# Dilated queries, keys and eight gate tiles as 2x2 block products with seven multiplications instead of eight

## The chip, the cores and the metric

The kernel runs on one core of one Trainium2 chip. The metric is the device time of one execution in microseconds (us). A core has five engines with an instruction stream each: TensorE (PE in the profile; its weight loads are listed as PEld), VectorE (DVE), ScalarE (ACT), GpSimd (POOL) and SyncE (SP), which issues the transfers here. Each runs its stream in order, and waits on semaphores for the others. Matrix products are made by PE into PSUM banks of 128 partitions x 512 float32; operands lie in SBUF.

## The reference

One layer of an encoder in float32, for one sequence of 1024 tokens and a width of 1024. `proj` is one input projection that is cut into ten parts: two mixers, their output gates z, and two merge gates g.

```python
h = rmsnorm(x, attn_norm_g)
c_q, c_kv, k_rope, z_mla, q_dil, k_dil, v_dil, z_dil, g_mla, g_dil = split(h @ w_in)
a_out = mla_attention(c_q, c_kv, k_rope, ...)          # 8 heads, dense, 1024 x 1024
y_mla = (a_out * silu(z_mla)) @ w_o_mla
d_out = dilated_mixture(rope(q_dil), rope(k_dil), v_dil)  # 3 groups x 8 heads of 64,
                                                       # windows 128, 512, 2048, dilations 1, 4, 16
y_dil = (d_out * silu(z_dil)) @ w_o_dil
merged = sigmoid(g_mla + b1) * y_mla + sigmoid(g_dil + b2) * y_dil
out = rmsnorm(x + merged @ w_out, final_norm_g)
```

## The kernel before

**Products.** Each float32 operand is split into a high part in the format fp32r and a low part, the rest (`split`, L73 to L76: a cast on ACT, L75, and a subtraction, L76, on POOL for weights and on DVE or POOL elsewhere). A product is three matmuls, high x high, low x high and high x low (`mm3`, L69 to L71; in a projection L70 takes the low part of the activations and L71 that of the weights). One mm3 of 128x512 is called a step here. A projection of one weight tile (128 output columns, a contraction of 1024 = 8 steps) for one half of the tokens (512) is eight steps into one bank.

**Stages.** The program goes through five stages; the times are those of the profiled execution. 0 to 241 us: latent projections, tables, norm factors, and the values of the dilated mixer (`dil_v`). 241 to 491 us: `dil_qk`, the dilated queries and keys, twelve calls of two weight tiles each, so 48 banks of 24 matmuls; a call makes for each half of the tokens two banks `pj`, rotates them (`rope`, four multiplications on DVE, L233, and two additions on POOL, L234 and L235), splits the result into `dq_st` for groups 0 and 1 (L75 and L76 on ACT and POOL) or copies it for group 2 (ACT, L397), and writes it to DRAM in pieces of 128 KB. 491 to 815 us: dilated attention, four head pairs of three groups each, and a combination of the groups per pair (`combine`). 815 to 1195 us: dense attention (`mla_attention`). 1195 us to the end: `output`.

**Fillers.** `fillers` (L415) is a generator of steps that don't depend on the attention at hand. It first makes the 24 tiles of z and of the gates, 16 steps each (numbers 4 to 7, 0 to 3, 16 to 23, 8 to 15; a DVE multiplication L428, a tanh on ACT, for z two POOL operations L431 and L432, a store to `s_zs` or `s_gt`), then the output projection of the dilated mixer (64 steps), then that of the dense mixer without its last quarter ("early" merges, three steps and a POOL addition for each of 16 pieces), as far as it gets before the attention ends. FIRST_FEED steps come ahead of the dilated attention; after that `feed(FEED[i])` draws steps from it after each group of scores or transposes: FEED[0] to FEED[5] in the dilated attention, FEED[6] and FEED[7] in the dense one. They use one PSUM bank, `pj`.

**Output.** For each of 16 pieces (8 tiles of columns x 2 halves of tokens) what is left of the dense mixer's projection is made: four steps, or one if the piece was early. DVE multiplies it by the gate (L830), POOL adds the dilated part (L831), ACT casts (`m`) and DVE subtracts (`mg_l`, L76). Beside each piece one of 16 parts of `w_out` is loaded (`wo_raw`) and split (ACT `wout_h`, DVE `wout_l`, L76). Then come 384 matmuls of 128x512 of the final product, the residual, the norm and the stores.

**Order.** The order in each engine's stream is set by a scheduler that takes the program as written, the free buffers of the pools and a model of times; it can bring an instruction forward past others of its engine. PSUM has eight banks: six and two for `pj` before the attention, and then two for transposes (`pt`), one for `av`, four for scores (`s_ps`) and one for `pj`. The attention takes over the banks when the pools of the stage before are closed.

## Time and profile before

| | us |
|---|---|
| median of 3 runs | 1338.19 (1333.47 to 1341.69) |
| profiled execution | 1334.28 |
| its span, first to last instruction | 1332.5 |
| 0 to 241: latents, tables, values | 241 |
| 241 to 491: queries and keys | 250 |
| 491 to 815: dilated attention | 324 |
| 815 to 1195: dense attention | 380 |
| 1195 to 1332.5: output | 137.5 |

The profiled execution is the basis of every sum; 1.8 us of it lie outside the span, and it is 3.9 us below the median. Rows of a table of windows give the stretch, its length, then for PE, PEld, DVE, ACT and POOL the busy time and the number of instructions, then the clock that PE was granted (1.00 is full), the mean busy share of the DMA engines and GB/s. Rows of groups give the line in the code, engine, operation, result and operands with shape, the count, the busy time, the mean duration in ns, and the idle time of that engine just before, with what ended it. Rows of a timeline give start, duration, instruction and the idle time before it.

### The profile page before, as it was taken

To read this page: it belongs to the slowest core of one execution; us is meant where nothing else is said; L and a number is where in the kernel's file an instruction comes from. 1 tells how busy PE (TensorE), PEld (TensorE's weight loads), DVE (VectorE), ACT (ScalarE), POOL (GpSimd) and SP (SyncE) were. 2 spreads that over 40 slices of the span, in tenths; PEclk is the share of its full clock that TensorE was granted. 3 is DMA by queue.
4 is the path that set the end of the run, shared out by engine and by line. 5 is a ranking of instruction groups with operands and counts; after the bars stand their busy time and mean duration, and the time that the engine had idled before them with its cause. 6 is when DMAs were issued, how large, how long until landed. Compare 5 with 4: busy or idle time off the path is not lost.

```text
span 1332.5 us, 19561 instructions
## 1 busy us (share of the span) xinstructions
PE 1275.5 (96%) x7101; PEld 1108.2 (83%) x7101; DVE 670.5 (50%) x1340; ACT 577.7 (43%) x1230; POOL 454.9 (34%) x302
## 2 busy tenths in 40 slices
PE   8999999999999999989999989999999999998998
PEld 8898999888888878877878777788888878886786
DVE  7473520222222215666475666766665666658622
ACT  6533332223322336545455453565555545454322
POOL 2251212676466634425422040312111022045522
PEclk9999999999999999989999999999999999999999
DMA  9758563575435435688777777625342463136322
GB/s 324 220 167 303 183 231 107 154 217 139 125 104 157 136 105 155 161 197 205 195 202 202 196 200 187 188 98 166 80 117 82 103 193 112 59 117 206 130 94 76
DMA packets 128256, 213.06 MB, mean 160 GB/s; under 512 B 36440, under 2 KB 65696, under 8 KB 126304
## 3 DMA queue, kind: packets, MB, share of 16 engines
q1 hardware_dynamic: 128160, 211.81, 54.8%
q8 instruction: 56, 0.92, 0.3%
q14 instruction: 40, 0.33, 0.1%
HBM read 143.01 MB, written 68.75 MB: 159 GB/s over the span
## 4 chain that ended last, share of the span: by engine, by line
PE 64%; DMA 12%; DVE 6%; issue 3%; SPq 2%; ACT 1%; POOL 0%; DVEq 0%; ACTq 0%; POOLq 0%
PE pj L69 15%; PE pj L71 15%; PE pj L70 15%; PE pt L546 3%; DMA op_a<-s_dk 2%; PE av L555 2%; PE av L554 2%; SPq L65 2%; DMA s_sd<-av_t 2%; PE s_ps L69 2%; PE s_ps L70 2%; PE s_ps L71 2%; PE pt L647 1%; DMA gate<-s_zs 1%; PE av L668 1%
## 5 line engine op out<-in xcount | busy, mean ns | idle before, releaser
L69 PE MATMUL pj<-hT_h,w_h 128*128 128x512 f32 x768 | 314.9, 410 | 2.2 <-DVE zg_z L428 2.1
L76 POOL TENSOR_TENSOR w_l<-w_raw,w_h 128x1024 fp32r<-128x1024 f32 (+1 forms) x70 | 167.8, 2399 | 434.6 <-ACT w_h L75 370.2
L71 PE MATMUL pj<-hT_h,w_l 128*128 128x512 f32 x768 | 301.8, 393 | 0.0
L70 PE MATMUL pj<-hT_l,w_h 128*128 128x512 f32 x768 | 301.7, 393 | 0.0
L233 DVE TENSOR_TENSOR rope_m<-pj,cs_d 128x512 f32<-128x512 f32 x96 | 61.8, 686 | 241.2 <-PE pj L71 241.2
L76 DVE TENSOR_TENSOR pt_l<-pt,pt_h 128x512 fp32r<-128x512 f32 x192 | 131.6, 686 | 87.9 <-ACT pt_h L75 86.3
L71 PEld LDWEIGHTS pj<-hT_h,w_l 128*128 128x128 f32 x768 | 145.4, 189 | 31.7
L69 PEld LDWEIGHTS pj<-hT_h,w_h 128*128 128x128 f32 x768 | 145.8, 190 | 27.7 <-DVE zg_z L428 3.0
L70 PEld LDWEIGHTS pj<-hT_l,w_h 128*128 128x128 f32 x768 | 146.2, 190 | 24.8
L75 ACT CAST pt_h<-pt 128x512 fp32r<-128x512 f32 x192 | 112.0, 584 | 116.5 <-PE pt L546 48.2
L70 PE MATMUL pj<-w_l,hT_h 128*128 128x256 f32 x384 | 109.2, 284 | 0.0
L71 PE MATMUL pj<-w_h,hT_l 128*128 128x256 f32 x384 | 109.0, 284 | 0.0
L69 PE MATMUL pj<-w_h,hT_h 128*128 128x256 f32 x384 | 109.0, 284 | 0.0
L75 ACT CAST w_h<-w_raw 128x1024 fp32r<-128x1024 f32 (+1 forms) x70 | 72.3, 1035 | 72.9 <-PE pj L70 59.4
L535 ACT ACTIVATE p<-s_ps,m_nm 128x512 f32<-128x512 f32 x128 | 87.4, 697 | 30.6 <-PE pt L546 19.1
L529 DVE TENSOR_REDUCE m_nm<-s_ps 128x1 f32<-128x512 f32 x128 | 86.6, 685 | 25.3 <-PE s_ps L71 23.1
L613 ACT ACTIVATE p<-p,d_st 128x256 f32<-128x256 f32 x128 | 64.4, 504 | 64.3 <-DVE d_st L612 64.1
L546 PE MATMUL pt<-consts,p 128*128 128x128 f32 x512 | 78.4, 276 | 4.1 <-ACT av_t L577 3.8
L612 DVE CUSTOM_DVE_ANT_0 p<-s_ps,masks 128x256 f32<-128x256 f32 x128 | 50.9, 416 | 47.7 <-PE s_ps L640 25.6
L69 PEld LDWEIGHTS pj<-w_h,hT_h 128*128 128x128 f32 x384 | 73.2, 191 | 1.1
L70 PEld LDWEIGHTS pj<-w_l,hT_h 128*128 128x128 f32 x384 | 73.3, 191 | 0.8
L71 PEld LDWEIGHTS pj<-w_h,hT_l 128*128 128x128 f32 x384 | 73.1, 190 | 0.7
(234 smaller groups left out, 2568.3 us busy)
## 6 DMA issues: line engine op xcount, KB each, us to landing
w_raw<-wt SPq DMA_DIRECT2D x48, 512.0 KB, 4.8
op_b<-s_dq SPq DMA_DIRECT2D x32, 512.0 KB, 8.6
s_dq<-dq_st SPq DMA_DIRECT2D x80, 128.0 KB, 2.5
s_dk<-dq_st SPq DMA_DIRECT2D x80, 128.0 KB, 2.5
gate<-s_gt SPq DMA_DIRECT2D x34, 256.0 KB, 3.1
s_dv<-dv_st SPq DMA_DIRECT2D x32, 256.0 KB, 4.6
s_gt<-zg_t SPq DMA_DIRECT2D x32, 256.0 KB, 2.7
w_raw<-wv SPq DMA_DIRECT2D x12, 512.0 KB, 5.7
```

Of the source, the lines that this page charges most:

```text
L65: self.nc.sync.dma_start(out=out, in_=in_)
L69: mm(out, lh, rh, start=start, stop=False)
L70: mm(out, lh, rl, start=False, stop=False)
L71: return mm(out, ll, rh, start=False, stop=stop)
L75: self.nc.scalar.copy(out=h, in_=raw)
L76: sub.tensor_tensor(out=l, in0=raw, in1=h.bitcast(F32), op=ALU.subtract)
L233: v.tensor_tensor(out=mi, in0=p, in1=tab, op=ALU.mult)
L529: v.tensor_reduce(out=nm[:, hh, qb, kb:kb + 1], in_=s, axis=AX.X, op=ALU.max, negate=True)
L535: nc.scalar.activation(out=p[:, 512 * kb:512 * kb + 512], in_=ss[kb], func=AF.Exp, bias=nm[:, hh, qb, 2:3], accum_out=den[:, hh, qb, kb:kb ...
L546: self.anchor = nc.tensor.transpose(pt[:, o:o + 128], P[b2][:, 128 * kc:128 * kc + 128], self.ident)
L612: nc.vector.tensor_tensor_reduce(out=p, in0=s, in1=mask, op0=ALU.add, op1=ALU.min, scale=-0.125, scalar=3e38, accum_out=nm)
L613: nc.scalar.activation(out=p, in_=p, func=AF.Exp, scale=-1.0, bias=nm, accum_out=den)
```

## The change

A pair of weight tiles, with its contraction cut into two halves of 512 and the tokens into two halves, is a 2x2 block product: each of four results (two tiles x two token halves) is the sum of two block products, eight in all. The changed kernel makes it by the Strassen-Winograd scheme: seven block products of four steps, on sums of blocks. `block_pair` does that for a pair: four sums of weight blocks on POOL, seven splits of a block of 128x512 (ACT cast, POOL subtraction, in place of two splits of 128x1024), seven products of 12 matmuls into four banks `st_a` to `st_d` (two sets of four, so all eight banks), three copies of a bank to SBUF on ACT, and five additions on DVE of which four are in place in PSUM. The sums of the activations, `s0` to `s3`, are made once by `block_sums`: the input is loaded again (16 loads of 256 KB), scaled on ACT, summed on POOL, and split on ACT and DVE.

The twelve calls of `dil_qk` use it, and so do gate tiles 8 to 15, as four pairs (ZG_PAIRS) behind calls 2, 5, 8 and 11; these eight tiles leave the fillers, and FEED is lowered. The rotation is now all on DVE and partly in place in PSUM (two multiplications to SBUF, two in place, two additions in place, for each half), the subtraction of the split of `dq_st` goes from POOL to DVE, and the stores of queries and keys are 512 KB each instead of 128 KB, 40 instead of 160. Weight tiles are split in halves of 128x512 throughout. `dil_v` is called in another order around `block_sums`, the scaling of the cosine and sine tables and the zeroing of a tile come earlier (both on POOL). In the changed file the lines of `mm3` are L71 to L73, the split's subtraction is L78, and the gate product L830 is L931.

```diff
-FEED = (1.9, 1.35, 1.2, 1.25, 2, 3, 1.1, 1.1)
+FEED = (1.4, 1.0, 0.9, 0.95, 1.5, 2.2, 0.95, 0.95)
...
+ZG_PAIRS = ((8, 2), (10, 5), (12, 8), (14, 11))
...
-        h = wp.tile([128, 8, 128], F32R, name="w_h")
-        l = wp.tile([128, 8, 128], F32R, name="w_l")
-        self.split(raw[:, :n], h[:, :n], l[:, :n], self.nc.gpsimd)
+        for k in range(0, n, 4):
+            m = min(4, n - k)
+            h = wp.tile([128, 4, 128], F32R, name="w_h", bufs=bufs)
+            l = wp.tile([128, 4, 128], F32R, name="w_l", bufs=bufs)
+            self.split(raw[:, k:k + m], h[:, :m], l[:, :m], self.nc.gpsimd)
+            w.append((h, l))
...
+    def block_sums(self, sp, tp):
 
         nc, a = self.nc, self.a
...
+        p = nc.gpsimd
+        self.sh = [sp.tile([128, 4, 512], F32R, name=f"s{i}_h") for i in range(4)]
+        self.sl = [sp.tile([128, 4, 512], F32R, name=f"s{i}_l") for i in range(4)]
+        for kc in range(4):
+            y = {}
+            for i in range(2):
+                for k in range(2):
+                    x = y[i, k] = tp.tile([128, 512], F32, name=f"y{i}{k}", bufs=2)
+                    c = kc + 4 * k
+                    self.dma(x, a["xt"][i, :, c])
+                    nc.scalar.mul(x, x, self.ga[:, c:c + 1])
+
+            p.tensor_tensor(out=y[1, 1], in0=y[1, 0], in1=y[1, 1], op=ALU.add)
+            p.tensor_tensor(out=y[1, 0], in0=y[0, 0], in1=y[1, 0], op=ALU.subtract)
+            p.tensor_tensor(out=y[0, 0], in0=y[1, 1], in1=y[0, 0], op=ALU.subtract)
+            p.tensor_tensor(out=y[0, 1], in0=y[0, 1], in1=y[0, 0], op=ALU.subtract)
+            for i, x in enumerate((y[1, 1], y[0, 0], y[1, 0], y[0, 1])):
+                self.split(x, self.sh[i][:, kc], self.sl[i][:, kc], nc.vector)
...
+    def block_pair(self, first, tp, pp):
+
+        nc, a = self.nc, self.a
+        p, v = nc.gpsimd, nc.vector
+        raw = []
+        for i, wp in enumerate((self.wp, tp)):
+            raw.append(wp.tile([128, 8, 128], F32, name="w_raw", bufs=2))
+            self.dma(raw[i], a["wt"][first + i])
+        b = {(k, i): raw[i][:, 4 * k:4 * k + 4] for k in range(2) for i in range(2)}
+        T = [tp.tile([128, 4, 128], F32, name=f"t{i}") for i in range(3)]
+        t1, t2, t4 = T
+        hx = lambda i, k: tuple(x[:, 4 * k:4 * k + 4, 512 * i:512 * i + 512] for x in (self.hTh, self.hTl))
+        sx = lambda i: (self.sh[i], self.sl[i])
+        ps = {n: pp.tile([128, 512], F32, name=f"st_{n}") for n in "abcd"}
+
+        def operand(x):
+            wp = (self.wp, self.wpx)[self.turn % 2]
+            self.turn += 1
+            h = wp.tile([128, 4, 128], F32R, name="w_h", bufs=4)
+            l = wp.tile([128, 4, 128], F32R, name="w_l", bufs=4)
+            self.split(x, h, l, p)
+            return h, l
+
+        def product(bank, x, act, start, stop=False):
+            h, l = operand(x)
+            for kc in range(4):
+                self.mm3(ps[bank], h[:, kc], l[:, kc], act[0][:, kc], act[1][:, kc], start and kc == 0, stop and kc == 3, skip=True)
+
+        def copied(bank):
+            x = tp.tile([128, 512], F32, name="st_c", bufs=2)
+            nc.scalar.copy(out=x, in_=ps[bank])
+            return x
+
+        product("a", b[0, 0], hx(0, 0), True)
+        product("b", b[1, 0], hx(0, 1), True, True)
+        p.tensor_tensor(out=t1, in0=b[0, 1], in1=b[0, 0], op=ALU.subtract)
+        product("c", t1, sx(0), True)
+        p.tensor_tensor(out=t2, in0=b[1, 1], in1=t1, op=ALU.subtract)
+
+        p.tensor_tensor(out=b[0, 1], in0=b[1, 1], in1=b[0, 1], op=ALU.subtract)
+        product("d", b[0, 1], sx(2), True)
+        u = copied("a")
+        v.tensor_tensor(out=ps["b"], in0=ps["b"], in1=u, op=ALU.add)
+        u = copied("c")
+        t = tp.tile([128, 512], F32, name="st_t")
+        v.tensor_tensor(out=t, in0=ps["d"], in1=u, op=ALU.add)
+        product("a", t2, sx(1), False, True)
+        product("c", b[1, 1], sx(3), False, True)
+        p.tensor_tensor(out=t4, in0=b[1, 0], in1=t2, op=ALU.subtract)
+        product("d", t4, hx(1, 1), False, True)
+        u = copied("a")
+        for bank, x in (("a", t), ("c", u), ("d", u)):
+            v.tensor_tensor(out=ps[bank], in0=ps[bank], in1=x, op=ALU.add)
+        return {(0, 0): ps["b"], (1, 0): ps["c"], (0, 1): ps["d"], (1, 1): ps["a"]}
...
+        out = self.block_pair(T_ZM + first, tp, pp)
+        for half in range(2):
+            for i in range(2):
+                self.zg_out(first + i, half, out[i, half], *(tp.tile([128, 512], F32, name=f"rope_m{n}") for n in range(2)))
...
-            pa, pb = self.proj_half(wa, half, pj), self.proj_half(wb, half, pj)
-            o = self.rope(pa, pb, self.cos_d[:, c512], self.sin_d[:, c512], tp)
+            pa, pb = o = out[0, half], out[1, half]
+            cos, sin = self.cos_d[:, c512], self.sin_d[:, c512]
+            m = [tp.tile([128, 512], F32, name=f"rope_m{i}") for i in range(2)]
+            for x, y in zip(m, (pb, pa)):
+                v.tensor_tensor(out=x, in0=y, in1=sin, op=ALU.mult)
+            for x in o:
+                v.tensor_tensor(out=x, in0=x, in1=cos, op=ALU.mult)
+            for x, y, op in zip(o, m, (ALU.subtract, ALU.add)):
+                v.tensor_tensor(out=x, in0=x, in1=y, op=op)
...
-                    self.split(o[c], st[c][0][:, c512], st[c][1][:, c512], nc.gpsimd)
+                self.split(src, dst[0], dst[1], v)
-                for j in range(4):
-
-                    self.dma(dst[quad * 4 + j, p, c, :, off:off + S], st[c][p][32 * j:32 * j + 32])
+                self.dma(dst[quad * 4:quad * 4 + 4, p, c, :, off:off + S], st[c][p])
...
-            for i in [4, 5, 6, 7, 0, 1, 2, 3, *range(16, 24), *range(8, 16)]:
+            for i in [4, 5, 6, 7, 0, 1, 2, 3, *range(16, 24)]:
...
+                            self.dil_v(0, 0, vp, pj)
+                            self.dil_v(0, 1, vp, pj)
+                    sp = sums.enter_context(tc.tile_pool(name="sums", bufs=1))
+                    with tc.tile_pool(name="bs", bufs=1) as tp:
+                        self.block_sums(sp, tp)
+                        self.dil_v(1, 0, vp, pj)
+                    for g, quad in ((1, 1), (2, 0), (2, 1)):
+                        self.dil_v(g, quad, vp, pj)
...
+                with tc.tile_pool(name="dt", bufs=1, side="right") as tp, tc.tile_pool(name="st", bufs=2, space=PSUM) as pp:
+                    zg, n = list(ZG_PAIRS), 0
+                    for quad in range(2):
+                        for g in range(3):
+                            for which in range(2):
+                                self.dil_qk(g, quad, which, tp, pp)
+                                n += 1
+                                if zg and zg[0][1] == n:
+                                    self.zg_pair(zg.pop(0)[0], tp, pp)
```

The first place in the order is DVE inside the stage of queries and keys. Before, its rows are the multiplications of `rope` alone (`pj` is a bank, `cs_d` the tables).

```order
L233 TENSOR_TENSOR rope_m_2531<-pj,cs_d 128x512
L233 TENSOR_TENSOR rope_m_2529<-pj,cs_d 128x512
L233 TENSOR_TENSOR rope_m_2530<-pj,cs_d 128x512
L233 TENSOR_TENSOR rope_m_2592<-pj,cs_d 128x512
L233 TENSOR_TENSOR rope_m_2595<-pj,cs_d 128x512
```

Of the changed program, a stretch that begins with the last operations of one pair and goes into the next; `st_a` to `st_d` are banks, except that `st_c` as a second operand in L444 and L447 is the copy in SBUF, and `st_t` lies in SBUF.

```order
L495 TENSOR_TENSOR st_d<-st_d,rope_m_4116 128x512
L444 TENSOR_TENSOR st_b<-st_b,st_c 128x512
L78 TENSOR_TENSOR dq_st_3964<-st_a,dq_st_3963 128x512
L491 TENSOR_TENSOR rope_m_4276<-st_b,cs_d 128x512
L78 TENSOR_TENSOR dq_st_3962<-st_d,dq_st_3961 128x512
L493 TENSOR_TENSOR st_b<-st_b,cs_d 128x512
L447 TENSOR_TENSOR st_t<-st_d,st_c 128x512
L454 TENSOR_TENSOR st_a<-st_a,st_t 128x512
L454 TENSOR_TENSOR st_c<-st_c 128x512
L491 TENSOR_TENSOR rope_m_4275<-st_c,cs_d 128x512
L493 TENSOR_TENSOR st_c<-st_c,cs_d 128x512
L495 TENSOR_TENSOR st_b<-st_b,rope_m_4275 128x512
```

The block's own additions (L444, L447, L454) stand among the rotation and the splits, and the read of the first `st_d` (L447), which the seventh product waits for, stands ahead of the pair's last additions.

The second place is PE where the stage ends and the first filler begins. Before:

```order
L69 MATMUL pj_4295<-hT_h_96,w_h_4199 128x512
L70 MATMUL pj_4295<-hT_l_97,w_h_4199 128x512
L71 MATMUL pj_4295<-hT_h_96,w_l_4200 128x512
L69 MATMUL pj_4364<-hT_h_96,w_h_4359 128x512 [waits Activation_49]
L70 MATMUL pj_4364<-hT_l_97,w_h_4359 128x512
L71 MATMUL pj_4364<-hT_h_96,w_l_4360 128x512 [waits Pool_49]
```

And of the changed program:

```order
L71 MATMUL st_d_5142<-hT_h_96,w_h_5250 128x512
L72 MATMUL st_d_5142<-hT_l_97,w_h_5250 128x512
L73 MATMUL st_d_5142<-hT_h_96,w_l_5251 128x512
L71 MATMUL pj_5324<-hT_h_96,w_h_5316 128x512 [waits DVE_49,PE_49,Activation_49]
L72 MATMUL pj_5324<-hT_l_97,w_h_5316 128x512
L73 MATMUL pj_5324<-hT_h_96,w_l_5317 128x512 [waits Pool_49]
```

The first filler's bank is now one that the last pair used, `st_d`: it waits for DVE and ACT to be done with it, where before it waited for its weight only.

The third place is DVE in the output, where the pieces end. Before:

```order
L830 SCALAR_TENSOR_TENSOR gate<-gate,pj 128x512 x2
L76 TENSOR_TENSOR mg_l<-gate,m_41_11846 128x512
L76 TENSOR_TENSOR mg_l<-gate,m_51_11870 128x512
L830 SCALAR_TENSOR_TENSOR gate<-gate,pj 128x512
L76 TENSOR_TENSOR mg_l<-gate,m_01_11885 128x512
```

And of the changed program:

```order
L931 SCALAR_TENSOR_TENSOR gate<-gate,pj 128x512
L78 TENSOR_TENSOR wout_l<-wo_raw,wout_h 128x512
L931 SCALAR_TENSOR_TENSOR gate<-gate,pj 128x512
L78 TENSOR_TENSOR mg_l<-gate,m_41_12500 128x512
L78 TENSOR_TENSOR wout_l<-wo_raw,wout_h 128x512
L78 TENSOR_TENSOR mg_l<-gate,m_51_12515 128x512
L78 TENSOR_TENSOR mg_l<-gate,m_61_12530 128x512
```

The number of these operations is the same, 16 of each kind; the splits of `w_out` now reach to the end of the sequence.

Counted in the two orders, in steps of three matmuls: the fillers put 240 steps into the dilated attention (with what precedes it) before and 184 after, 214 and 181 into the dense attention, and the output is left with 58 and 19. Of the 16 pieces 2 were early, and 15 are now.

111 lines of the change are left out of this document (54 added, 57 removed).

## The prediction

> **What bounds the kernel now.** I read the page first: span and busy time.
>
> ```profile
> span 1332.5 us, 19561 instructions
> PE 1275.5 (96%) x7101; PEld 1108.2 (83%) x7101; DVE 670.5 (50%) x1340; ACT 577.7 (43%) x1230; POOL 454.9 (34%) x302
> ```
>
> PE is busy for 96%, only 57 us are idle. The average hides stages with different limits, so next come the windows of the five stages (columns as told above).
>
> ```profile
> core 0: us, PE busy (x) PEld busy (x) DVE busy (x) ACT busy (x) POOL busy (x), PEclk, DMA share, GB/s
> 491.00:815.00 324.00, 300.66 (x1774) 262.59 (x1773) 191.26 (x482) 168.07 (x421) 107.96 (x85) 0.97 0.74 193
> 815.00:1195.00 380.00, 370.05 (x2098) 318.59 (x2098) 244.77 (x438) 205.01 (x460) 71.00 (x44) 0.99 0.42 120
> 1195.00:1332.50 137.50, 126.20 (x565) 102.14 (x564) 69.62 (x114) 41.32 (x85) 55.25 (x37) 0.99 0.39 130
> 241.00:491.00 250.00, 250.00 (x1105) 207.01 (x1104) 59.24 (x92) 68.37 (x84) 154.00 (x100) 1.00 0.51 140
> ```
>
> Queries and keys are PE and nothing else: 250 of 250 us. In the dilated attention PE is idle for 23 us, the DMA engines work at 0.74. How much of the fillers there holds up the end is told by the chain of waits of each stage:
>
> ```profile
> by line: PE pj L69 9.9%; DMA op_a<-s_dk 9.6%; PE pj L71 9.4%; PE pj L70 9.4%; SPq L65 6.1%; DMA s_sd<-av_t 5.5%; issue 5.2%; PE pt L647 5.1%; PE av L668 4.3%; PE s_ps L703 3.3%; PE s_ps L639 3.0%; DMA op_b<-s_dq 3.0%; DMA bc<-s_rr 2.9%; PE
> by line: PE pt L546 12.1%; PE pj L69 10.8%; PE pj L71 10.6%; PE pj L70 10.6%; PE av L555 6.9%; PE av L554 6.6%; PE s_ps L69 5.8%; PE s_ps L70 5.7%; PE s_ps L71 5.7%; DMA gate<-s_zs 3.9%; issue 2.8%; DVE m_nm L529 2.3%; DMA zg_t<-s_zs 2.1%;
> ```
>
> The first line is 491 to 815 us: the fillers' `pj` are 9.9 + 9.4 + 9.4 = 28.7% of 324, 93 us. The second is 815 to 1195: 10.8 + 10.6 + 10.6 = 32% of 380, 121.6 us. The rest is attention, loads and issue, which the change doesn't shorten. All 240 steps there are 240 x 0.675 = 162 us of PE work (0.675 below), so over a third of them fill time that would pass anyway.
>
> **The change, part by part.** The prices of the block stage:
>
> ```profile
> 250.00:300.00 50.00, 50.00 (x222) 41.42 (x221) 11.59 (x18) 12.01 (x14) 36.42 (x24) 1.00 0.81 217
> L233 DVE TENSOR_TENSOR rope_m<-pj,cs_d 128x512 f32<-128x512 f32 x96 | 61.8, 686 | 241.2 <-PE pj L71 241.2
> L726 DVE COPY num<-av 128x512 f32<-128x512 f32 x8 | 8.3, 1035 | 16.2 <-PE av L724 13.9 <-PE pt L750 2.2
> L234 POOL TENSOR_TENSOR rope_m<-rope_m,rope_m 128x512 f32<-128x512 f32 x26 | 33.6, 1294 | 88.4 <-DVE rope_m L233 88.4
> L831 POOL TENSOR_TENSOR gate<-gate,m 128x512 f32<-128x512 f32 x16 | 24.9, 1574 | 20.6 <-DVE gate L830 12.7 <-issue 6.6 <-ACT m L75 1.3
> L75 ACT CAST dq_st<-rope_m 128x512 fp32r<-128x512 f32 x32 | 27.9, 872 | 91.7 <-POOL rope_m L234 66.6 <-POOL rope_m L235 24.5
> L397 ACT COPY dq_st<-rope_m 128x256 f32<-128x256 f32 x32 | 18.9, 640 | 48.2 <-POOL rope_m L234 43.0 <-POOL rope_m L235 4.8
> ```
>
> *Block stage.* 222 matmuls in 50 us are 0.225 us each. Before, 48 banks x 24 matmuls x 0.225 = 259.2 us; after, 16 pairs x 84 x 0.225 = 302.4, because four gate pairs join: **+43.2 us**, if PE stays the bound. A pair gives the others 18.9 us. A pair of group 0 or 1 has 21 DVE operations (8 for the rotation's products, 4 for its sums, 4 subtractions, 5 block additions): x 0.686 = 14.4 us. No row shows DVE writing PSUM; L233 reads it, and the dearest DVE row that reads it is the copy L726 at 1.035: 21.7 us. I take 0.686, the same operation with one operand in PSUM. POOL has 4 sums and 7 subtractions: 11 x 1.294 = 14.2, at the 1.574 of L831 17.3. ACT has 7 casts, 4 more for the split and 3 copies: 14 x 0.872 = 12.2 at the dearer row. All three lie under 18.9. On SP's queue a pair has two loads of 512 KB as before, and 8 stores instead of 32 (4 instead of 16 in group 2), or 4 of 256 KB for the gates, whose loads and stores leave the attention's queue. The new waits lie on PE: the seventh product needs DVE's read of the first `st_d` (L447 in the order), queued on DVE behind the rotation of the pair before. It has two products, 2 x 12 x 0.225 = 5.4 us, of slack, and half a DVE queue of 14.4 us can be behind it without a wait, as the banks are doubled. Behind the waiting matmul stands the next pair; nobody else waits.
>
> *Sums, tables, zeros.* The 16 POOL additions are 16 x 1.294 = 20.7 to 16 x 1.574 = 25.2 us, behind loads and ACT's scaling, beside some of POOL's weight splits. The cover is what is left of the value products on PE (370 matmuls of 128x256 in the order) and the first two block products, which use no sums:
>
> ```profile
> 200.00:240.00 40.00, 40.00 (x278) 37.47 (x277) 2.58 (x4) 9.16 (x16) 12.14 (x7) 1.00 0.36 116
> ```
>
> 40/278 = 0.144 us each, so 53 us and 5.4. I take 0; if loads, ACT and DVE take turns with POOL instead of overlapping, up to 8 us come out. Table scaling and zeros sit in the same cover.
>
> *End of the block stage.* The first filler waits for the last `st_d`: behind the last matmul come about seven DVE operations (7 x 0.686 = 4.8) and two ACT copies (2 x 0.640), with the last matmul's own 0.39 us about 7 us idle. Queued behind on PE are the 19 first steps and the first head's scores, on which DVE and ACT then wait. What such a gap does to the clock:
>
> ```profile
> 501.41 0.39 PE L639 MATMUL s_ps<-op_a,op_b 128*128 128x256 f32 x1 [2.65 <-DVE d_st L612]
> 574.84 0.36 PE L639 MATMUL s_ps<-op_a,op_b 128*128 128x256 f32 x1 [4.54 <-DMA op_b<-s_dq]
> 576.00:578.00 2.00, 2.00 (x12) 2.00 (x11) 0.74 (x4) 1.50 (x6) 0.00 (x0) 0.50 1.04 206
> 578.00:580.00 2.00, 2.00 (x11) 2.00 (x11) 0.00 (x0) 0.00 (x0) 0.00 (x0) 0.50 1.13 198
> 580.00:582.00 2.00, 2.00 (x7) 1.57 (x7) 1.05 (x1) 0.00 (x0) 0.00 (x0) 0.53 0.85 199
> 582.00:584.00 2.00, 2.00 (x13) 1.65 (x11) 0.43 (x2) 0.60 (x2) 0.00 (x0) 1.00 0.89 340
> ```
>
> After 4.54 us idle the clock was 0.50 for some 6 us, 3 us lost. So 7 + 3, less the 2.65 us that PE now waits at 501 for scores and which the gap swallows: **+7** (0 if other work is brought forward, 10 if nothing is swallowed). The Trainium skill, "TensorE: Matmul & The Clock Gate", Part 1: The HAM clock gate, has the array at half rate after an idle window of about 3.4 us, and at full rate after about 3.4 us of work. By that the loss would be 1.7 us and the term 6; the half rate agrees, the trace's 6 us are longer than the page's figure.
>
> *Dilated attention.* 56 of 240 steps go, 56 x 3 x 0.225 = 37.8 us of PE work. The chain holds 93 us of the fillers' 162: 93 x 56/240 = **-21.7**. Bounds: 10 (rival 2, below) and 37.8. The chain is that of before: as soon as a filler is gone, the next of the loads or DVE's softmax can be late, so I take the share that it shows and not the whole.
>
> *Dense attention.* 33 of 214 steps go, 22.3 us; by the chain 121.6 x 33/214 = **-18.8** (12 to 22.3). That stage has 10 us of idle PE, so most of it should show.
>
> *Output.*
>
> ```profile
> L830 DVE SCALAR_TENSOR_TENSOR gate<-gate,pj 128x512 f32<-128x512 f32 x16 | 10.5, 675 | 0.0
> L76 DVE TENSOR_TENSOR mg_l<-gate,m 128x512 fp32r<-128x512 f32 x16 | 20.0, 1256 | 1.5 <-ACT m L75 1.2
> L76 DVE TENSOR_TENSOR wout_l<-wo_raw,wout_h 128x512 fp32r<-128x512 f32 x16 | 16.8, 1062 | 7.9 <-ACT wout_h L75 7.9
> L71 PE MATMUL pj<-wout_h,mg_l x136: 279/392/393, 1237.5 to 1325.8; 128*128 128x512 f32 x120, 128*128 128x256 f32 x16
> L76 DVE TENSOR_TENSOR mg_l<-gate,m x16: 677/1246/1781, 1209.6 to 1247.8; 128x512 fp32r<-128x512 f32 x16
> 1256.00:1320.00 64.00, 64.00 (x278) 52.03 (x277) 18.69 (x47) 13.63 (x36) 15.55 (x12) 1.00 0.30 100
> 1198.49 0.63 ACT wout_h L75
> ```
>
> 39 fewer steps, 117 matmuls x 0.225 = 26.3 us. But DVE's 48 operations remain: 10.5 + 20.0 + 16.8 = 47.3 us, and they can't begin before the first cast, `wout_h` at 1198.49 (the chain's row), so they end at about 1246 on before's clock. Before, PE had pieces to make until the first `mg_l` matmul at 1237.5, so DVE was nearly hidden. After, PE has 19 steps, 13 us, and the final product could begin at 1215; but its second bank already needs the other column half of `w_out`, whose splits reach to the end of DVE's row (third place in the order). By the order 69 of the 384 matmuls can run ahead of the last splits: 1246 less one to three operations of 1.1, then 315 x 0.2302 (64/278), then the tail of 6.7 (1332.5 - 1325.8), is 1322 to 1325. I take 1323.5, **-9**. The bounds are -2, if `mg_l` runs at its 1.781, since 16 x 0.5 = 8 us more on DVE eat most of it, and -14, if it runs at 0.677 for half of the 16 (8 x 0.58 = 5). The 13 more early pieces put a DVE multiplication (0.675) and a POOL addition (1.574) each into the dense attention, 9 and 20 us in a stage where DVE is busy for 245 of 380 and POOL for 71: nothing.
>
> *Sum:* 43.2 + 7 - 21.7 - 18.8 - 9 = +0.7, so 1335.0 against 1334.3; on the median's scale (3.9 more) **1339 us**. PE's own work falls by 128 steps x 0.675 - 43.2 = 43.2 us: what the seven products save comes back as waits.
>
> **Rivals.** *1, faster: the attention gives back all its fillers.* PE is 93 and 97% busy there, which speaks for it; the loads in its chain (9.6, 5.5, 3.0%) speak against. 43.2 + 7 - 37.8 - 22.3 - 9 = -18.9: 1319; with all the output's 26.3 also, 1302.
>
> *2, no change to slower: DVE and transfers pace the dilated attention.* Stretches of the second of the four head pairs (324/4 = 81 us each):
>
> ```profile
> 570.00:580.00 10.00, 5.46 (x27) 5.20 (x26) 2.10 (x8) 2.63 (x9) 2.52 (x2) 0.75 1.05 228
> 585.00:600.00 15.00, 15.00 (x95) 13.31 (x94) 14.62 (x42) 10.90 (x31) 5.57 (x4) 1.00 0.62 160
> 605.00:615.00 10.00, 6.68 (x34) 5.33 (x33) 9.29 (x18) 5.24 (x14) 7.61 (x5) 0.88 0.80 214
> 615.00:630.00 15.00, 15.00 (x90) 13.29 (x89) 7.29 (x22) 7.97 (x23) 8.54 (x9) 0.97 1.07 258
> 650.00:660.00 10.00, 8.33 (x46) 7.24 (x45) 3.63 (x9) 4.67 (x12) 4.88 (x3) 0.85 1.02 219
> ```
>
> In 25 of the 81 us DVE is full (14.62 of 15, 9.29 of 10), in another 35 the DMA share is over 1.0. If a filler taken out there only leaves a gap, what is left is 21/81 of 37.8, 10 us: 1339 + 21.7 - 10 = 1351. Against it: PE has no gap at 585 to 600 and at 615 to 630, so work there did wait for PE. It decides once the idle time of PE in the stage grows by more than half of the 37.8.
>
> *3, slower: DVE bounds the block pairs.* At 1.035 a pair of groups 0 and 1 takes 21.7 us instead of 18.9, and then PE waits at `st_d`: 8 such pairs x 2.8 = 22.5, so 1361. It decides from a mean of 18.9/21 = 0.90 us. For it: DVE writes PSUM, which no row shows, and in the output `mg_l` takes 677 to 1781 ns beside POOL's additions. Against: POOL is busy for 36.42 of 50 us beside L233, and that stays at 686. The Trainium skill, "SBUF — State Buffer", Who interferes with whom, says that a DVE instruction contends with a GpSimd one that reads SBUF only if both of its inputs are in SBUF. The pair's 21 have one in PSUM each, so by the page they keep L233's price and this rival falls; the rows agree as far as they go.
>
> That the change doesn't do what it says is excluded by the order: 84 matmuls for each pair.
>
> **How the numbers follow.** One per cent, 13.4 us, is about what a measurement of this kernel can tell from no change. Forecast 0.36 (0.30 within 1%, 0.03 on either side), rival 1 0.33 (0.31 faster, 0.02 within), rival 2 0.15 (0.10 within, 0.05 slower), rival 3 0.16 (0.02 within, 0.14 slower). Faster 0.34, same 0.44, slower 0.22. The range goes from rival 1 with all the output gains, 1302, to rival 3: 1303 to 1360.
>
> **What would show it.** Right: PE without a gap through the 16 pairs in 302 us, DVE's in-place rows near 690 ns; one wait of about 7 us on `pj` behind it, at half clock after; a dilated attention of 302 us and a dense one of 361, with more idle PE in the first; `wout_l` as what PE waits for in the output. Wrong: DVE rows of 0.9 us or more in the pairs, gaps at the first sums, or attention stages shorter by 38 and 22 us.

## The result, and the profile after

The changed kernel takes 1423.2 us (median of 4 runs, 1414.89 to 1430.55) against 1337.88 for the kernel before: a ratio of 1.0648, 95% interval 1.0605 to 1.069. It is slower by 6.5%, where no change was forecast, and lies 63 us above the range.

First the page of the changed kernel: span, busy time, and the chain that ended last.

```profile
span 1428.8 us, 19809 instructions
PE 1279.4 (90%) x6909; PEld 1096.0 (77%) x6909; DVE 793.4 (56%) x1528; ACT 637.2 (45%) x1428; POOL 550.3 (39%) x434
PE 48%; DMA 27%; DVE 7%; issue 3%; ACT 3%; SPq 3%; POOL 3%; ACTq 0%; DVEq 0%; POOLq 0%
```

PE is busy as long as before (1275.5) with 192 matmuls fewer, part of them at half clock, and is idle for 149 us instead of 57. In the chain, transfers have gone from 12% to 27%. The windows say where: those of the kernel before, cut at the last value product, the first scores of each attention and the last scores (the dilated attention's row, 491 to 815, stands in the prediction), then those of the changed kernel, cut at its first block product and then at the same events (columns as in the prediction).

```profile
225.00:492.00 267.00, 267.00 (x1182) 221.14 (x1181) 61.82 (x96) 72.32 (x90) 162.38 (x104) 1.00 0.51 141
815.00:1173.00 358.00, 348.36 (x1974) 299.99 (x1974) 230.69 (x415) 194.21 (x441) 62.46 (x38) 0.99 0.43 121
1173.00:1332.50 159.50, 147.90 (x689) 120.75 (x688) 83.70 (x138) 52.12 (x105) 63.80 (x42) 0.99 0.37 125
```

```profile
228.00:619.00 391.00, 336.58 (x1368) 268.17 (x1368) 171.40 (x272) 128.19 (x243) 226.00 (x178) 0.93 0.35 116
619.00:940.00 321.00, 274.65 (x1607) 239.76 (x1606) 192.40 (x476) 161.02 (x420) 102.29 (x92) 0.91 0.75 190
940.00:1283.00 343.00, 329.68 (x1882) 284.06 (x1881) 225.79 (x418) 188.21 (x441) 71.94 (x58) 0.98 0.44 124
1283.00:1428.80 145.80, 126.59 (x560) 100.25 (x559) 83.24 (x137) 49.10 (x103) 62.37 (x44) 0.94 0.38 128
```

The block stage has grown by 124 us, and by 129 with the gap of 4 us ahead of it; 50 were forecast. PE, which never waited there, is idle for 54 us of it, at a clock of 0.93, and the DMA engines are *less* busy than before, 0.35 instead of 0.51. The three stages behind give back some 2, 15 and 14 us. So the loss is in the block stage. Its chain, and the longest waits on DVE, ACT and PE in it (instruction, what it waited for, us in total, times, longest):

```profile
by line: DMA s_dq<-dq_st 22.8%; DMA s_gt<-rope_m 22.4%; DMA s_dk<-dq_st 4.1%; SPq L67 3.9%; PE st_a L71 3.9%; PE st_c L71 3.8%; PE st_c L72 3.7%; PE st_c L73 3.7%; PE st_a L72 3.5%; PE st_a L73 3.5%; PE st_d L71 3.0%; issue 2.9%; PE st_d L7
```

```profile
DVE rope_m L468 <- ACT rope_m L475: 65.0, 8, 17.5
DVE dq_st L78 <- DMA s_dq<-dq_st: 43.0, 4, 12.0
ACT rope_m L475 <- DMA s_gt<-rope_m: 76.9, 12, 19.8
PE st_a L71 <- ACT st_c L432: 30.3, 5, 11.4
PE st_c L71 <- ACT st_c L432: 17.2, 4, 4.8
```

PE waits for ACT's copies of banks, ACT stands at a tile from which a gate is still being stored, DVE at a staging tile `dq_st` that is still being stored. Half of the stage's chain is three stores. How long one takes, by the chain in order of time (start, duration), and what the DMA engines do meanwhile:

```profile
296.88 18.40 DMA s_gt<-rope_m
340.80 22.17 DMA s_dq<-dq_st
```

```profile
298.00:302.00 4.00, 4.00 (x19) 3.33 (x18) 0.62 (x1) 0.00 (x0) 3.82 (x4) 1.00 0.26 105
308.00:312.00 4.00, 0.93 (x4) 0.40 (x3) 0.00 (x0) 0.00 (x0) 0.00 (x0) 0.92 0.25 104
312.00:314.00 2.00, 0.00 (x0) 0.00 (x0) 0.00 (x0) 0.00 (x0) 0.00 (x0) 0.50 0.26 107
```

Every engine stands still at 312, and the DMA engines work at a quarter, 0.25 to 0.26, at some 105 GB/s. It is not that there is much to move: the 512 KB stores use four of sixteen engines. The packet records of the traces show it directly: from 308 to 312 us four packets, nearly all of 4 KB and 0.159 us, are under way at almost any moment; while the kernel before issues 128 KB stores (490 to 494 us), it is about sixteen, of the same size and duration. A pair of groups 0 and 1 stores 2 MB, 20 us at that rate; the pool `dt` has its staging tiles once (bufs=1, before 2), so the next pair's split waits for them, and a gate's 256 KB store stands behind the 2 MB. That was the theory (A) for the experiments. Its rivals were the single tiles by themselves (B), and the chain of copies on ACT by itself (C).

### The profile page after: what moved, and what is told of

It reads as the page before. It is cut to its first block, busy times and chain, and to the rows that moved or that the text cites. A ratio compares the mean times of both kernels' runs of the same rounds, so it can differ in the third digit from the quotient of the medians.

```text
span 1428.8 us, 19809 instructions
## 1 busy us (share of the span) xinstructions
PE 1279.4 (90%) x6909; PEld 1096.0 (77%) x6909; DVE 793.4 (56%) x1528; ACT 637.2 (45%) x1428; POOL 550.3 (39%) x434
## 4 chain that ended last, share of the span: by engine, by line
PE 48%; DMA 27%; DVE 7%; issue 3%; ACT 3%; SPq 3%; POOL 3%; ACTq 0%; DVEq 0%; POOLq 0%
PE pj L71 7%; PE pj L72 7%; PE pj L73 7%; DMA s_dq<-dq_st 6%; DMA s_gt<-rope_m 6%; PE pt L647 3%; SPq L67 3%; DMA op_a<-s_dk 2%; PE av L656 2%; DMA op_b<-s_dq 2%; PE av L655 2%; PE s_ps L71 1%; PE s_ps L72 1%; PE s_ps L73 1%; PE pt L748 1%
## 5 line engine op out<-in xcount | busy, mean ns | idle before, releaser
L78 POOL TENSOR_TENSOR w_l<-w_raw,w_h 128x512 fp32r<-128x512 f32 (+1 forms) x140 | 182.2, 1309 | 411.6 <-ACT w_h L77 346.6
L78 DVE TENSOR_TENSOR pt_l<-pt,pt_h 128x512 fp32r<-128x512 f32 x192 | 131.3, 685 | 62.9 <-ACT pt_h L77 61.6
L71 PE MATMUL pj<-hT_h,w_h 128*128 128x512 f32 x256 | 115.1, 450 | 7.2 <-ACT dq_st L507 5.4
L77 ACT CAST w_h<-w_raw 128x512 fp32r<-128x512 f32 (+1 forms) x140 | 84.3, 613 | 62.9 <-PE st_d L72 19.4
L73 PE MATMUL pj<-w_h,hT_l 128*128 128x256 f32 x384 | 108.9, 284 | 0.0
L71 PE MATMUL pj<-w_h,hT_h 128*128 128x256 f32 x384 | 108.6, 283 | 0.0
L72 PE MATMUL pj<-hT_l,w_h 128*128 128x512 f32 x256 | 104.1, 407 | 0.0
L73 PE MATMUL pj<-hT_h,w_l 128*128 128x512 f32 x256 | 103.7, 405 | 0.0
L636 ACT ACTIVATE p<-s_ps,m_nm 128x512 f32<-128x512 f32 x128 | 87.3, 696 | 22.3 <-PE pt L647 16.8
L656 PE MATMUL av<-pt_l,op_c 128*128 128x256 f32 x256 | 68.3, 290 | 6.4 <-DVE pt_l L78 6.3
L73 PEld LDWEIGHTS pj<-w_h,hT_l 128*128 128x128 f32 x384 | 73.4, 191 | 0.9
L71 PEld LDWEIGHTS pj<-w_h,hT_h 128*128 128x128 f32 x384 | 73.4, 191 | 0.8
L740 PE MATMUL s_ps<-op_a,op_b 128*128 128x256 f32 x128 | 42.0, 341 | 33.8 <-DVE d_st L713 14.2
L655 PE MATMUL av<-pt_h,op_c 128*128 128x256 f32 x256 | 70.7, 291 | 1.2 <-ACT pt_h L77 1.2
L647 PEld LDWEIGHTS pt<-consts,p 128*128 128x128 f32 x512 | 61.7, 143 | 11.0 <-ACT av_t L678 6.1
```

The lines of the kernel that those rows point to most:

```text
L71: mm(out, lh, rh, start=start, stop=False, skip_group_check=skip)
L72: mm(out, lh, rl, start=False, stop=False, skip_group_check=skip)
L73: return mm(out, ll, rh, start=False, stop=stop, skip_group_check=skip)
L77: self.nc.scalar.copy(out=h, in_=raw)
L78: sub.tensor_tensor(out=l, in0=raw, in1=h.bitcast(F32), op=ALU.subtract)
L636: nc.scalar.activation(out=p[:, 512 * kb:512 * kb + 512], in_=ss[kb], func=AF.Exp, bias=nm[:, hh, qb, 2:3], accum_out=den[:, hh, qb, kb:kb ...
```

## The experiments

The table gives each run's stages, cut as above (us; the first is from the last value product to the first scores), and the matmul steps that the fillers put into the dilated attention.

| kernel | time, median | queries and keys | dilated | dense | rest | steps |
|---|---|---|---|---|---|---|
| before | 1338 | 266.7 | 323.4 | 357.4 | 159.8 | 232 |
| changed | 1423.2 | 395.4 | 320.6 | 343.7 | 145.3 | 176 |
| e1, small stores | 1358.3 | 334.3 | 309.9 | 344.4 | 145.7 | 176 |
| e2, gate tile doubled | 1407.8 | 381.9 | 316.0 | 342.0 | 146.0 | 176 |
| e10, stores of two heads | 1612.9 | 576.4 | 319.4 | 343.5 | 146.0 | 176 |
| e4, before with big stores | 1353.0 | 266.7 | 336.2 | 356.7 | 159.7 | 232 |
| e13, before with stores of two heads | 1532.8 | 395.1 | 392.7 | 359.1 | 159.7 | 232 |
| e5, gates as fillers | 1332.5 | 256.7 | 336.8 | 361.0 | 157.5 | 232 |
| e7, all gates in pairs | 1389.0 | 411.6 | 290.1 | 313.0 | 150.3 | 117 |
| e6, e1 with other banks | 1355.6 | 330.2 | 309.4 | 343.7 | 145.7 | 176 |
| e9, e5 with other banks | 1333.7 | 254.8 | 333.3 | 359.4 | 157.4 | 232 |
| e12, e5 without sums as operands | 1326.0 | 256.7 | 327.6 | 357.8 | 157.2 | 232 |
| e14, e5 with staging tiles apart | 1329.7 | 255.0 | 334.0 | 358.9 | 156.9 | 232 |

**e1: the stores alone, as before.**

```diff
-                self.dma(dst[quad * 4:quad * 4 + 4, p, c, :, off:off + S], st[c][p])
+                for j in range(4):
+                    self.dma(dst[quad * 4 + j, p, c, :, off:off + S], st[c][p][32 * j:32 * j + 32])
```

> The changed kernel, only its stores of queries and keys again in four parts of 32 partitions (128 KB each). Theory A (a store of 512 KB runs on a quarter of the DMA engines, at some 104 GB/s, so that a pair's 2 MB take 20 us, and the single set of staging tiles makes the next pair wait for them): the block stage falls from about 385 us to 302 to 325, the total from 1423 to 1340 to 1365. Theory B (the single set of staging tiles is enough of a cause: any store has to land before the next split): the stage stays above 350, the total at 1390 or more. Theory C (ACT's copies and PE's waits for them, the transfers being a symptom): no change, 1415 to 1425.

1358.31 us, ratio to before 1.0153 (1.0117 to 1.0189). PE's order in the block stage is the same to the last instruction; only the form of the forty transfers differs, now 160. Its window:

```profile
227.00:557.60 330.60, 322.80 (x1369) 260.57 (x1370) 172.16 (x272) 131.25 (x244) 227.99 (x178) 0.98 0.47 138
```

PE is idle for 8 us instead of 54, with the single staging tiles still in place. 61 of the stage's us went with the form of the stores, and another 11 came back in the dilated attention (320.6 to 309.9; e4 tells why). The total is where A had it. B and C fall as causes by themselves: the same tiles and the same copies do no harm when a store is quick.

**e2: a second tile for the gates.** The changed kernel with its big stores, and the tile from which a gate is stored doubled (the rotation uses the same tile, so its line changes too).

```diff
-                self.zg_out(first + i, half, out[i, half], *(tp.tile([128, 512], F32, name=f"rope_m{n}") for n in range(2)))
+                self.zg_out(first + i, half, out[i, half], *(tp.tile([128, 512], F32, name=f"rope_m{n}", bufs=1 + n) for n in range(2)))
...
-            m = [tp.tile([128, 512], F32, name=f"rope_m{i}") for i in range(2)]
+            m = [tp.tile([128, 512], F32, name=f"rope_m{i}", bufs=1 + i) for i in range(2)]
```

> The changed kernel with its stores of 512 KB, only the tile from which a gate is stored is double (2 KB more). Theory A: a gate's store is late because it stands behind 2 MB of queries and keys; more tiles let ACT run ahead by one, but the 2 MB still hold the next pair's split: 1395 to 1423, the wait for the dq_st stores stays. If it is the gate's single tile that makes the pairs late, the stage falls by 50 us or more, to under 1375.

1407.76 us, 1.0519 (1.0471 to 1.0568): 15 us better, as far as A allowed. More room lets ACT run ahead by a step, but DVE's wait for the stores of `dq_st` is as long as in the changed kernel, 43.1 us in total after 43.0. More room for `dq_st` itself, a second set of tiles, was not run in the changed kernel.

**e10 and e13: half as many heads in a store.** A store of two heads, 256 KB, in the changed kernel and, with double staging tiles, in the kernel before.

```diff
-                for j in range(4):
-                    self.dma(dst[quad * 4 + j, p, c, :, off:off + S], st[c][p][32 * j:32 * j + 32])
+                for j in (0, 2):
+                    self.dma(dst[quad * 4 + j:quad * 4 + j + 2, p, c, :, off:off + S], st[c][p][32 * j:32 * j + 64])
```

> The changed kernel with its stores in two parts of two heads, 256 KB each. If a store is spread over as many DMA engines as its destination has heads in the outermost place (four of sixteen gave a share of 0.25): single stores show a share near 0.13, the pair's 2 MB take 20 us or more, and the time is 1400 or above. If the size of a transfer is what matters: halfway, 1375 to 1395, with shares over 0.25.

> The kernel before, with double staging tiles, its stores of queries and keys in two parts of two heads (256 KB). Theory A (a store runs on as many DMA engines as heads stand outermost, here two, at some 52 GB/s): a pair of groups 0 and 1 needs 2 MB / 52 GB/s = 40 us, one of group 2 20 us, against 21.6 us of PE; the stage becomes 8 x 40 + 4 x 21.6 = 406 us or less, where stores of group 0 and 1 run on under group 2: 360 to 410 instead of 266, the total 1435 to 1490. If only a single set of staging tiles makes the stores harmful: as with one part, 1340 to 1365.

1612.91 us (1.2059, 1.2017 to 1.2102) and 1532.77 (1.1459, 1.1426 to 1.1492). Windows of e10, with the DMA share in the column before the last:

```profile
312.00:316.00 4.00, 4.00 (x19) 3.31 (x18) 1.38 (x2) 0.00 (x0) 4.00 (x4) 1.00 0.13 53
316.00:320.00 4.00, 4.00 (x20) 3.28 (x19) 0.00 (x0) 0.00 (x0) 1.35 (x2) 1.00 0.12 51
320.00:324.00 4.00, 4.00 (x19) 3.22 (x18) 0.00 (x0) 0.00 (x0) 0.00 (x0) 1.00 0.13 53
```

0.13 is two of sixteen, at half of the rate of four, and two packets are under way at a time, where four were. A store of 256 KB is slower than one of 512 KB, and one of 128 KB with 32 rows outermost faster than both, so the size isn't what matters: the heads in the outermost place of the destination set the number of engines, 26 GB/s each. And e13 shows that double tiles help only while the stores of a pair take less time than its products: at 40 us against 21.6 the stage went to 395 us, within the 360 to 410 expected. Its total, 43 us above what was expected, has more in it that stands behind the stores in SP's queue: weights for the next pair come late (ACT's wait), and after the stage the first softmax waits for the masks, whose load is issued at 692 us, and PE with it.

```profile
ACT w_h L75 <- DMA w_raw<-wt: 194.8, 17, 20.1
PE s_ps L638 <- DVE d_st L611: 75.5, 3, 71.7
```

**e4: the kernel before with the big stores.**

```diff
-                for j in range(4):
-
-                    self.dma(dst[quad * 4 + j, p, c, :, off:off + S], st[c][p][32 * j:32 * j + 32])
+                self.dma(dst[quad * 4:quad * 4 + 4, p, c, :, off:off + S], st[c][p])
```

> The kernel before, only its stores of queries and keys in one part of 512 KB instead of four of 128 KB; its staging tiles are double. Theory A: the stores of a pair need 20 us of a pair's 21.6 us of PE, two sets of tiles hide that: 1338 to 1350, with a DMA share of about 0.25 more often. If the form of the store alone does the harm, without the single tiles, the stage of queries and keys grows from 250 to over 300 us and the total to over 1385.

1353.01 us, 1.0118 (1.008 to 1.0155), 3 us above A's range. The stage itself didn't change, 266.7 us: 20 us of stores hide under 21.6 us of products when the tiles are double. The 13 us are in the dilated attention, at its beginning. PE's longest wait there, in the kernel before and then in e4:

```profile
PE s_ps L639 <- DVE d_st L612: 5.6, 5, 2.7
PE s_ps L637 <- DVE d_st L610: 17.4, 4, 15.7
```

DVE, in its turn, waits for the masks there. SP's queue in the kernel before, then in e4:

```profile
490.20 3.57 SPq L65 DMA_DIRECT2D s_dk<-dq_st  x8
495.99 0.35 SPq L65 DMA_DIRECT2D masks<-masks  x1
```

```profile
491.82 0.51 SPq L65 DMA_DIRECT2D s_dk<-dq_st  x1
509.66 0.33 SPq L65 DMA_DIRECT2D masks<-masks  x1
```

The load of the masks waits for the closed staging pool (e14 shows that it is this pool), until the last stores have landed: to 496 before, to 510 here. So the big stores cost in two places, and with double tiles the first cost is gone. But e4's pairs last 21.6 us and those of the changed kernel 18.9; whether double tiles would hide 20 us of stores there too was not run.

**e5: block products for queries and keys alone.** e1, with gate tiles 8 to 15 as fillers again and the old rates.

```diff
-ZG_PAIRS = ((8, 2), (10, 5), (12, 8), (14, 11))
+ZG_PAIRS = ()
-FEED = (1.4, 1.0, 0.9, 0.95, 1.5, 2.2, 0.95, 0.95)
+FEED = (1.9, 1.35, 1.2, 1.25, 2, 3, 1.1, 1.1)
-            for i in [4, 5, 6, 7, 0, 1, 2, 3, *range(16, 24)]:
+            for i in [4, 5, 6, 7, 0, 1, 2, 3, *range(16, 24), *range(8, 16)]:
```

> The changed kernel with the stores in four parts, and without the gate pairs: gate tiles 8 to 15 are fillers again, with the rates before; the seven products stay for the twelve pairs of queries and keys. Theory A: the stage takes 12 x 18.9 = 227 us instead of 250, with about 7 us at its end, the attention and the output are as before: 1338 - 32 + 7 = 1313, within 1305 to 1325. Theory B: the pairs stay at 24 us and more, 1360 to 1390. If moving the gates pays, this is slower than the changed kernel with stores in four parts; if the dilated attention has a pace of its own, it is faster by 25 us or more.

1332.47 us, 0.997 (0.9948 to 0.9992): 26 us better than e1, but 7 us above what was expected of it (most of it in the dilated attention, which was taken to be as before and is 13 us longer; see e14). So moving the gates costs: by the table four gate pairs add 78 us to the stage, and take 27 from the dilated attention, 17 from the dense one and 12 from the rest.

**e7: all sixteen gate tiles in pairs.** e1 with four more pairs and lower rates; the fillers keep the z tiles and what follows.

```diff
-ZG_PAIRS = ((8, 2), (10, 5), (12, 8), (14, 11))
+ZG_PAIRS = ((8, 2), (10, 3), (12, 5), (14, 6), (16, 8), (18, 9), (20, 11), (22, 11))
-FEED = (1.4, 1.0, 0.9, 0.95, 1.5, 2.2, 0.95, 0.95)
+FEED = (0.9, 0.64, 0.58, 0.61, 0.96, 1.4, 0.6, 0.6)
...
-            for i in [4, 5, 6, 7, 0, 1, 2, 3, *range(16, 24)]:
+            for i in [4, 5, 6, 7, 0, 1, 2, 3]:
...
-                                if zg and zg[0][1] == n:
+                                while zg and zg[0][1] == n:
```

> The changed kernel with the stores in four parts, and with all sixteen gate tiles made as eight block pairs; the fillers keep the z tiles and the output projections, and the rates fall with them. Four more pairs add 4 x 19.5 = 78 us to the block stage and take 128 steps, 87 us of work, out of the attention and the output. If the attention gives back fillers at the share seen between the kernels with and without the first four gate pairs (52 us for 78): 1380 to 1390. If it gives back all: 1349 to 1355. If it has reached a pace of its own: 1400 or more, with PE's idle time in it grown by 60 us.

1388.96 us, 1.0385 (1.0359 to 1.041), as expected for a share like that of the first four pairs. Another 77 us of block stage, and 20, 31 and -5 us back. The price of a pair is constant; the share of it that comes back falls. In the dilated attention, at 3 x 0.2267 = 0.68 us a step: from 232 to 176 steps 27 of 38 us come back (71%), from 176 to 117 20 of 40 (49%). In the dense attention 28 steps fewer (200 to 172, up to the last scores) gave back 17 of 19 us, and 81 fewer (to 91) 31 of 55. The idle time shows in the windows of the dilated attention, of e1 and then of e7, with PE idle for 39 and for 50 us, and the clock at 0.93 and 0.89:

```profile
557.60:867.50 309.90, 270.45 (x1606) 235.37 (x1605) 190.60 (x476) 161.12 (x420) 102.20 (x92) 0.93 0.76 196
```

```profile
632.80:923.00 290.20, 239.89 (x1427) 211.79 (x1426) 183.48 (x467) 150.68 (x404) 90.81 (x83) 0.89 0.78 193
```

**e6 and e9: another order of the banks.** So that the first filler's bank is `st_b`, which is done first.

```diff
-        ps = {n: pp.tile([128, 512], F32, name=f"st_{n}") for n in "abcd"}
+        ps = {n: pp.tile([128, 512], F32, name=f"st_{n}") for n in "acdb"}
```

> The changed kernel with the stores in four parts (1358 us), and with the four banks of a pair laid out in the order a, c, d, b, so that the first filler's bank is the one whose results are done first. If the wait at the end of the block stage is a matter of that bank: the 5.4 us wait for the copies of dq_st and the 3 us of half clock behind it go, first scores 8 us earlier, total 1349 to 1352. If the load of the masks, which waits for the last stores, ends last there anyway, the wait only moves to the first scores: 1355 to 1359.

> The kernel with block products for the queries and keys only, gates as fillers, stores in four parts (1332 us), and the banks in the order a, c, d, b. If the bank holds up the end of the stage: 1323 to 1327, faster than before by 0.8 to 1.1%. If the masks do: 1330 to 1334.

1355.62 us (1.0137, 1.0115 to 1.0158) and 1333.66 (0.9976, 0.9956 to 0.9996): against e1 and e5 no difference that these runs can tell. PE's wait at the end of the stage, on `pj` (the second line), is 5.4 us in e9 as in e1, e5 and e6:

```profile
PE s_ps L741 <- DVE d_st L714: 6.5, 1, 6.5
PE pj L71 <- ACT dq_st L507: 5.4, 1, 5.4
```

In the timeline of e9 it ends at 470.1 us with the last copy, out of `st_d`; `st_b` was last read at 465.3. That the filler's bank is that of `st_b` here is worked out from the order in which the banks are laid out; no record names the bank. So as far as these runs show, the handover is by pool, not by bank: no new tile is written before all of the old pool's readers are done. The second branch of each expectation has the right time, but its picture was wrong as well: the wait didn't move. The load of the masks waits for the pool of the staging tiles in the same way (e4, e14).

**e14: the staging tiles in a pool of their own.** e5, so that the masks' memory belongs to a pool that the last stores don't read.

```diff
-        st = [[tp.tile([128, S], F32R if g < 2 else F32, name=f"dq_st{c}{p}") for p in range(parts)] for c in range(2)]
+        st = [[self.dqs.tile([128, S], F32R if g < 2 else F32, name=f"dq_st{c}{p}") for p in range(parts)] for c in range(2)]
...
-                with tc.tile_pool(name="dt", bufs=1, side="right") as tp, tc.tile_pool(name="st", bufs=2, space=PSUM) as pp:
+                with tc.tile_pool(name="dt", bufs=1, side="right") as tp, tc.tile_pool(name="dqs", bufs=1, side="right") as self.dqs, tc.tile_pool(name="st", bufs=2, space=PSUM) as pp:
```

> The kernel with block products for queries and keys only, gates as fillers and stores in four parts (1332 us), with the staging tiles in a pool of their own, so that the memory of the masks no longer waits for the last stores; in the order the load of the masks now stands ahead of the last eight stores and waits for none. If the wait for the masks is a part of what the dilated attention lost (336.8 and 333.3 us against 323.3 before with as many fillers): the wait of 6 to 7 us at the first scores goes, the dilated attention takes 326 to 331, the total 1324 to 1328, faster than before by 0.7 to 1%. If something else sets it: 1331 to 1334.

1329.67 us, 0.9938 (0.9913 to 0.9963): the fastest version here that computes everything, 0.6% below the kernel before. Its interval overlaps with that of e5, so these runs don't tell the two apart. The time lies between the two forecasts, and the dilated attention above the 326 to 331 of the first. SP's queue in e14:

```profile
465.92 7.92 SPq L67 DMA_DIRECT2D w_raw<-wt  x1
473.96 0.36 SPq L67 DMA_DIRECT2D masks<-masks  x1
474.41 9.38 SPq L67 DMA_DIRECT2D s_dk<-dq_st  x8
```

The masks go ahead of the stores now, but stand behind a weight load whose issue takes 8 us. PE's wait at the first scores is 4.3 us instead of 5.9. The dilated attention takes 334.0 us, 2.8 less than e5 and still 10.6 more than before with as many fillers:

```profile
476.00:810.00 334.00, 305.73 (x1774) 266.10 (x1773) 193.04 (x483) 169.44 (x435) 112.91 (x98) 0.95 0.73 192
```

Against the row of before (492 to 815: 299.66 busy, at 0.97) PE is idle for some 5 us more, and busy for 6 us more with the same steps at the lower clock, 0.95. Which gaps throw the clock back there, and why there are more of them, stays open.

**e12: what the sums cost as operands.** e5, with blocks of the input in place of the sums, so it leaves out the sums and its queries and keys are not the right ones.

```diff
-        sx = lambda i: (self.sh[i], self.sl[i])
+        sx = lambda i: hx(i % 2, i // 2)
```

> The kernel with block products for queries and keys only (1332 us), whose products of activation sums take blocks of the normalised input itself in place of the sums, so queries and keys are not the right ones; every instruction and its size stay. Matmuls on sums took 0.231 to 0.237 us from start to start, those on the input 0.227. If the tiles of the sums are the cause (where they lie or what is in them): all at 0.227, the block stage 4 to 5 us shorter. If it is the products' place in the pair, with the work of other engines beside it: unchanged, 0.231 to 0.237.

1326.01 us, 0.9913 (0.9879 to 0.9948). The same stretch of the block stage in e5 and in e12:

```profile
260.00:440.00 180.00, 180.00 (x780) 146.21 (x779) 115.31 (x186) 72.79 (x138) 135.79 (x106) 1.00 0.54 153
```

```profile
260.00:440.00 180.00, 180.00 (x796) 149.10 (x795) 119.38 (x193) 74.37 (x141) 140.19 (x110) 1.00 0.60 174
```

PE makes 2% more matmuls in the same time: the start of the next one comes after 0.2267 us throughout, instead of a mean of 0.231. So the tiles of the sums are the cause, not their place in the pair. The stage as a whole was no shorter, 256.7 us, since PE waited 5 us longer for weights at its beginning in the profiled execution (7.9 us instead of 2.6).

## Why the prediction was wrong, point by point

**The step that failed** is the one on SP's queue in the block stage: "a pair has two loads of 512 KB as before, and 8 stores instead of 32". It counted issues, and gave the stores no duration. Its premise, that a larger transfer of the same bytes is no dearer, was not in any row. The page of the profile of before has these stores in the old form alone, 2.5 us from issue to landing for 128 KB with 32 rows outermost, and none with four heads outermost:

```profile
s_dq<-dq_st SPq DMA_DIRECT2D x80, 128.0 KB, 2.5
```

The runs show in its place: 512 KB with four heads outermost go at 104 GB/s on four engines, so a pair's 2 MB take 20 us, longer than its 18.9 us of products, and the next pair's split waits for the staging tiles. That these are single, `bufs=1` in the diff, was not priced either. e1 puts 61 us on the form of the stores in the stage, e1 and e4 some 11 to 13 us more behind it. The Trainium skill, "DMA: Bandwidth & Descriptors", "Why a DMA increments its semaphore by 16 and not by 1", states the rule: a transfer is spread over the largest number of engines up to 16 that divides the slowest dimension on both sides. Four heads make four, two make two, 32 rows sixteen; the shares of 0.25 and 0.13 and the packets under way agree with it. Read against the diff, and with the 26 GB/s of an engine measured here, it would have given 20 us of stores for each pair, and a rival with a price. None of the three rivals was this one.

**Block stage without that, +43.2 and +7.** e1 has 334.3 us against 266.7, so +67.6 in place of +50.2. DVE was right, and rival 3 falls: in-place operations in PSUM cost no more than others, 0.69 to 0.70 us against its 1.035. From the changed kernel:

```profile
L454 DVE TENSOR_TENSOR st_a<-st_a,st_t 128x512 f32<-128x512 f32 x16 | 11.2, 700 | 19.6 <-ACT st_c L432 18.9
L493 DVE TENSOR_TENSOR st_a<-st_a,cs_d 128x512 f32<-128x512 f32 x12 | 8.3, 689 | 0.0
```

POOL was as priced, 1.29 to 1.33, and ACT cheaper, 0.59 to 0.62 against 0.872. Of the 17 us, some 6 are the slower matmuls on sums (1344 x 0.0045, e12), and some 9 the other handover, at the start of the stage: in e1 PE waits there for 3.5 us (for ACT's copies of the last value banks), 1.3 and 0.6 (for weight casts), and runs at a clock of 0.85 over 20 us:

```profile
220.00:240.00 20.00, 14.21 (x62) 10.90 (x62) 8.14 (x8) 7.82 (x15) 11.38 (x9) 0.85 0.26 87
```

The prediction took 0 for that start, with up to 8 if the sums came late; they came in time, the banks and the weights didn't. By the chain a weight tile was loaded only after the last values had been stored. Here it is in the changed kernel, where the stage starts in the same way:

```profile
227.81 2.07 DMA s_dv<-dv_s
230.01 3.48 DMA w_raw<-wt
233.87 1.29 POOL t L437
```

The wait at the end was predicted as 7 us idle and half clock behind it, for the bank of the last `st_d`; it was 5.4 and half clock behind it, so right in size, but it ends with the last reader of the whole pool (e9).

**Dilated attention, -21.7.** Measured -2.8, and -13.5 in e1. The share by the chain, 57%, lies between the two measured, 71% from e5 to e1 and 49% from e1 to e7. What was missing is a price for its beginning, where the masks wait for the last stores, and for the lower clock: e5, with all its fillers, is 13.4 us slower there than the kernel before. So -26.9 of the fillers and +13.4 make the -13.5 of e1, and the big stores take 10.7 of that away. Neither rival 1 (all 37.8) nor rival 2 (10 us, with DVE or the transfers as the pace) is what happened. Rival 2's sign, idle time of PE that grows by more than half of the 37.8, is there in the changed kernel (23 to 46 us), but not where the fillers alone differ: from e5 to e1 it grows by 10 us, from 30 to 39.

**Dense attention, -18.8, and output, -9.** The table cuts these two at the last scores, the prediction later, at the end of the attention. Cut there, at the last `av` (1190.5 us before, 1299.6 after), where the prediction's counts of 33 and 39 steps hold, the dense attention gave back 15.2 us and the output 12.8: both within their bounds of 12 to 22.3 and 2 to 14, the output near the far one, as `mg_l` ran faster than assumed. The rows of the changed kernel:

```profile
L78 DVE TENSOR_TENSOR mg_l<-gate,m x16: 677/682/1779, 1309.6 to 1350.1; 128x512 fp32r<-128x512 f32 x16
L78 DVE TENSOR_TENSOR wout_l<-wo_raw,wout_h x16: 676/1170/1784, 1307.6 to 1347.8; 128x512 fp32r<-128x512 f32 x16
```

Its median fell from 1246 to 682 ns. The splits of `w_out` do last to the end there, as the prediction had it.

**Sum.** With e1's stores the change comes out at 1358, 19 us above the forecast, for the block stage's 17 us and the attention's beginning. That this lies just inside the range, and near rival 3's 1361, is luck: the range ends there for dearer DVE operations, and they weren't dearer. That most of what the seven products save is lost elsewhere was right, and it holds for queries and keys alone: e5 has 144 matmuls fewer than the kernel before, 33 us at 0.2267, and is only 0.3% faster, with the masks freed (e14) 0.6%; waits take part of it, slower matmuls and a lower clock the rest.

## What to carry to other kernels

Price a store by what it is made of, not by its issue: here the outermost dimension of the destination decided how many DMA engines carried it, and fewer and larger transfers ran on a quarter or an eighth of the engines. Where a change merges transfers *and* cuts the buffers that they read from, work out for each period how long the transfer takes against the work that hides it. Work moved out of a stage that it fills returned only a share, near the one that the stage's chain shows, and a smaller one the second time, so compare the price of a moved piece (19.4 us here) with that share of it and not with all of it.
